# Where the plain chunks stand between the products of a Strassen-like block, norm weights stored on 128 partitions, and a load queue changed

## The chip, the cores and the metric

The kernel runs on one NeuronCore of a Trainium2 chip. The metric is the device time of one execution in microseconds (us), from the first instruction to the last with what the program needs around them. The input arrays lie in HBM in the layout that the host code prepares, and that preparation is not timed.

## The reference, cut to what matters

The reference is two transformer blocks on one sequence of 256 tokens and width 1024, in float32:

```python
x = x + 0.5 * swiglu(rms_norm(x, g), w_gate, w_up, w_down)    # width 2816, first of four such layers
...
x = x + first_mixer(rms_norm(x, g))       # sparse attention and pooling; q and k: rms_norm per head, with q_norm, k_norm
x = x + 0.5 * swiglu(...)                 # second
x = x + 0.5 * swiglu_2(...)               # third
x = x + hybrid_mixer(rmsnorm(x, g), ...)  # with a norm of its own, sgu_norm
x = x + 0.5 * swiglu_2(...)               # fourth
return rmsnorm(x, final_norm)
```

where `swiglu(h) = (silu(h @ w_gate) * (h @ w_up)) @ w_down`. The four feed-forward layers (called FFN 1 to 4 here) are most of the time.

## The kernel before, in words

**Precision.** A float32 matrix is used as two parts of a faster matmul type: `split` makes the high part by a copy on ScalarE (line 82, ACT) and the low part by a subtraction on VectorE (line 83, DVE). `mm3` (lines 88 to 90) multiplies them as hi·hi, hi·lo and lo·hi. Every weight chunk of 128x2048 values is loaded, split into tiles `whi` and `wlo` (three buffers of each, in the pool `wsp`) and used by TensorE (PE). So the split of a chunk can start only when the third chunk before it has been used.

**Plain chunks.** `weights` loads a chunk into `raw` (two buffers, SP queue), splits it, and `rows` multiplies it for both halves of the tokens: 24 matmuls of 512 columns. These results go to PSUM banks with the tag `acc` (five).

**7-product blocks.** `quad` computes a 2x2 block product (two token halves, gate and up columns, two halves of the inner dimension) with seven products in place of eight. A product is 12 matmuls of 512 columns into a PSUM bank with the tag `tmp` (three banks, which the transposes in `turned` use too). The seven are, in order of `yield`: p1 of quarter w11; p2 of w12, which holds the sum of two quarters; p3 of w22; p4 of w21; p5 of w11 with another quarter added to it; p6 after `w11 += w22` on DVE (line 198); p7 after `w11 += w21` on DVE (line 201). The sums for p2 and p5 are made by adding DMAs (`more`, line 180, POOL queue). The quarters lie in tiles `block` (four buffers) and were loaded by the POOL queue (line 156). Results of p1, p2, p3 and p5 leave PSUM by an ACT copy (line 177), the others by a DVE operation (lines 193, 199, 207). When p7 is done, a few DVE sums (204 to 207, 393), `silu` and `gated` make the layer's hidden values, which `turned` transposes on PE and splits.

**Order.** The string `ORDER` names the steps of one FFN after its first group of columns: `e` (2 plain chunks) and `4` (4 plain chunks) are groups of columns computed plainly, `a`, `b` and `c` are three 7-product blocks, 7 steps each, and `d` is the down product (13 steps: 12 chunks, the last in two). After each step, work put off by `later` may be issued. The tile framework takes the program in this order, and sets each engine's own order of instructions and the buffers when the kernel is built; engines then run their queues in order.

**The mixers.** In the first, lines 456 to 479 load tables and form `C` and `S` from `cosq`, `sinq` and the head norm `g`, which was read from a [1, 64] array and broadcast to 128 partitions by the DMA (line 467, SP queue). `sgu_norm` (line 733, POOL queue) and `final` (line 287, SP queue) were broadcast in the same way from [1, 1024].

Of the kernel before, what the change touches and what calls it, by code (L numbers as in the profile page):

```python
# [17 lines left out]
P = 128  # L18
T = 256
D = 1024  # L20
# [3 lines left out]
HD = 64  # L24
# [9 lines left out]
WARM = 14  # L34


ORDER = "eeaa4aa4a4aa4bbdbbdbbdbccdccdcdcdcdddddd"
DOWN = ((0, 0), (0, 5), (0, 4), (1, 0), (1, 5), (1, 4), (0, 1), (1, 1), (0, 2), (1, 2), (0, 3), (1, 3))


class Block:
# [108 lines left out]
        yield  # L150
        self.split(dst[:, :, 0, :], dst[:, :, 1, :], s)

    def block(self, src=None):
        b = self.blocks.tile([P, 2048], F32, tag="block", name="block")
        if src is not None:
            self.nc.gpsimd.dma_start(b, src)
        return b

    def quad(self, pool, b, x, xc):


        nc, tt = self.nc, self.nc.vector.tensor_tensor
        of_x = lambda c, t: lambda k: self.both(x[:, 4 * c + k, :, t * P : t * P + P])
        of_xc = lambda i: lambda k: self.both(xc[:, 4 * i + k, :, :])

        def product(left, w):
            ps = self.bank("tmp")
            for k in range(4):
                c = slice(k * 512, k * 512 + 512)
                self.mm3(ps, left(k), (w[0][:, c], w[1][:, c]), k == 0, k == 3)  # L170
            return ps

        p = lambda tag: pool.tile([P, 512], F32, tag=tag, name=tag)

        def copy(ps, tag):
            y = p(tag)
            nc.scalar.activation(y, ps, AF.Copy)
            return y

        more = lambda w, src: nc.gpsimd.dma_start(w, src, accum_op=ALU.add)  # L180
        (b11, b12), (b21, b22) = b
        w12 = self.block(b12)
        more(w12, b22)
        w11, w22, w21 = self.block(b11), self.block(b22), self.block(b21)
        y11 = copy(product(of_x(0, 0), self.parts(w11)), "p1")
        more(w11, b12)
        yield
        p7 = copy(product(of_xc(2), self.parts(w12)), "p7")
        yield
        y12 = copy(product(of_xc(3), self.parts(w22)), "p3")  # L190
        yield
        y21 = p("p2")
        tt(y21, product(of_x(1, 0), self.parts(w21)), y11, op=ALU.add)
        y11, v = y21, y11
        yield
        p5 = copy(product(of_xc(0), self.parts(w11)), "p5")
        yield
        tt(w11, w11, w22, op=ALU.add)  # L198
        tt(v, product(of_xc(1), self.parts(w11)), v, op=ALU.subtract)
        yield  # L200
        tt(w11, w11, w21, op=ALU.add)  # L201
        w = self.parts(w11)
        ps = product(of_x(1, 1), w)
        tt(p7, p7, v, op=ALU.add)
        tt(v, v, p5, op=ALU.add)
        tt(p5, p7, p5, op=ALU.add)
        tt(p7, ps, p7, op=ALU.subtract)
        return y11, p7, y12, v, p5
# [74 lines left out]
    def ending(self):  # L283

        nc = self.nc
        self.fg = self.block()[:, :D]
        nc.sync.dma_start(self.fg, self.a["final"].to_broadcast([P, D]))
        self.half = self.small.tile([P, 2], F32, tag="tot", name="half")
        nc.vector.tensor_scalar(self.half, self.sq[:, 0, :], 1.0 / D, EPS, op0=ALU.mult, op1=ALU.add)
        self.y = [self.block()[:, :D] for _ in range(2)]  # L290
        for t in range(2):
            nc.vector.tensor_tensor(self.y[t][:, :512], self.X[t][:, :512], self.fg[:, :512], op=ALU.mult)
# [55 lines left out]
    def ffn(self, n, following, first=False):  # L348
        nc, a = self.nc, self.a
        gu, d, d_end = a[f"gu{n}"], a[f"d{n}"], a[f"de{n}"]  # L350
        with self.stage(4), self.tc.tile_pool(name="act", bufs=1) as pool:
            act = pool.tile([P, KF, 2, T], F32R, tag="act", name="act")
            xc = pool.tile([P, 16, 2, P], F32R, tag="xc", name="xc")
# [32 lines left out]
                gated(j, sgs, [x[:, T:] for x in G] if j == 5 else U)  # L386

            def seven(j):
                y11, y21, y12, x, y22 = yield from self.quad(pool, [[gu[2 * j + i, c] for i in range(2)] for c in range(2)], self.hT, xc)

                def rest():
                    tt = nc.vector.tensor_tensor
                    tt(y12, y12, x, op=ALU.add)
                    gated(j, silu([y11, y21]), [y12, y22])

                self.later(rest, 3)
# [40 lines left out]
            next(combined)  # L437

            steps = {"a": seven(1), "b": seven(2), "c": seven(3), "4": eight(4), "e": eight(5), "d": down()}
            for step in ORDER:  # L440
                next(steps[step], None)
# [14 lines left out]
    def mixer1_tables(self):  # L456
        nc, a, c1 = self.nc, self.a, self.c1
        load = lambda name, shape, engine=None: self.load(c1, name, shape, engine)
        self.cosi, self.sini = load("cosi", [P, 2, 32]), load("sini", [P, 2, 32])
        cosq, sinq = load("cosq", [P, 2, 64]), load("sinq", [P, 2, 64])  # L460
        self.causal, self.ncausal = load("causal", [P, 2, T], nc.gpsimd), load("ncausal", [P, 2, T], nc.gpsimd)
        self.band, self.pw = load("band", [P, 4, 384], nc.gpsimd), load("pool_w", [P, 4, P], nc.gpsimd)
        self.pscale = load("pool_scale", [P, 4], nc.gpsimd)
        self.heads_of = {}
        for n in ("q", "k"):
            g = c1.tile([P, HD], F32, tag=f"{n}g", name=f"{n}g")
            nc.sync.dma_start(g, a[f"{n}_norm"].to_broadcast([P, HD]))
            self.heads_of[n] = (cosq, sinq, g)

    def tables_of(self, n):  # L470
# [258 lines left out]
    def mixer2_tables(self):  # L729
        load = lambda name, shape: self.load(self.c2, name, shape, self.nc.gpsimd)  # L730
        self.sw, self.sb, self.cw = load("sgu_w", [P, 8, P]), load("sgu_b", [P, 8]), load("conv_w", [P, 8, 3])
        self.sn = self.c2.tile([P, D], F32, tag="sn", name="sn")
        self.nc.gpsimd.dma_start(self.sn, self.a["sgu_norm"].to_broadcast([P, D]))

    def mixer2(self, following):
        nc, a, m2 = self.nc, self.a, self.m2
# [127 lines left out]
    def load(self, pool, name, shape, engine=None):  # L864
        t = pool.tile(shape, F32, tag=name, name=name)
        (engine or self.nc.sync).dma_start(t, self.a[name])
        return t
# [70 lines left out]
def _layout(i):  # L938
    i = {k: np.asarray(v) for k, v in i.items()}
    one = {k: (v[0] if k not in ("x", "final_norm_2") else v) for k, v in i.items()}  # L940
    out = {"x": i["x"][0].reshape(2, P, D), "xT": i["x"][0].T.reshape(KD, P, T).transpose(1, 0, 2)}
    downs = [one["ffn1_w_down"], one["ffn2_w_down"], one["ffn1_w_out_2"], one["ffn2_w_out_2"]]
    gates = [(one[f"ffn{s}_w_gate"], one[f"ffn{s}_w_up"]) for s in "12"]
    gates += [(w[:, :FF], w[:, FF:]) for w in (one["ffn1_w_in_2"], one["ffn2_w_in_2"])]
    for n, (gu, w) in enumerate(zip(gates, downs), 1):
        out[f"gu{n}"] = _gate_up(*gu)
        out[f"d{n}"] = _chunks(w[: 20 * P])
        out[f"de{n}"] = np.stack([_by_rows(w[20 * P :, f * 512 : f * 512 + 512], 2)[0] for f in range(2)])
    w = one["w_in"]
    q, k, v, qi, ki, wi, u = np.split(w, np.cumsum([512, 512, 512, 256, 64, 4]), axis=1)  # L950
    out["w_idx"] = _by_rows(np.concatenate([qi, ki, wi], 1), 4)
    for n, m in (("q", q), ("k", k), ("v", v), ("u", u)):
        out[f"w_{n}"] = _by_rows(m, 4)
    out["w_out"] = np.concatenate([_chunks(one["w_out"][:512])[:, 0], _chunks(one["w_out"][512:])[:, 0]])
    out["pool_w"] = one["pool_w"].transpose(1, 0, 2)
    out["pool_scale"] = one["pool_scale"].reshape(4, P).T
    w = one["w_in_2"]
    u, v, gb, gc, xb, ga, gbb = np.split(w, 7, axis=1)
    for n, m in (("w_v2", v), ("w_u2", u), ("w_ga2", ga), ("w_gb2", gbb), ("w_pa2", one["w_proj_a_2"]),
                 ("w_pb2", one["w_proj_b_2"]), ("w_out_2", one["w_out_2"])):  # L960
        out[n] = _chunks(m)
    out["w_b2"] = _by_tile(gb).reshape(4, 2, P, D).transpose(0, 2, 1, 3).reshape(4, P, 2 * D)
    out["w_cx"] = _by_tile(gc, xb)
    out["sgu_w"] = one["sgu_w_2"].transpose(2, 0, 1)
    out["sgu_norm"] = one["sgu_norm_2"].reshape(1, D)
    out["sgu_b"] = one["sgu_b_2"].T
    out["conv_w"] = one["conv_w_2"].reshape(3, 8, P).transpose(2, 1, 0)
    out["final"] = one["final_norm_2"].reshape(1, D)
    out["gains"] = np.concatenate([one[n].reshape(KD, P).T for n in NORMS], 1)
    for n in ("q_norm", "k_norm"):  # L970
        out[n] = one[n].reshape(1, HD)
    return {k: np.ascontiguousarray(v) for k, v in out.items()}


# [9 lines left out]
```

## Time and profile before

| | us |
|---|---|
| median of 3 runs (lowest, highest) | 1111.79 (1111.42, 1115.6) |
| the profiled execution | 1109.44 |
| its span, first to last instruction | 1107.7 |
| PE busy in the span | 1067.8 (96%) |
| DVE busy | 818.4 (74%) |
| ACT busy | 605.3 (55%) |
| mean granted TensorE clock | 0.989 |

The profiled execution lies 2.35 us below the median, and its span 1.74 us below its own time. "Busy" of PE counts matmuls whose ends are modelled and which overlap, so what PE loses is read from the distance of matmul starts and from the idle times that the rows name.

### The profile page before, as it was taken

The numbers are of one execution on the slowest core, as the hardware profiler recorded it, in microseconds if no ns is written. First come the engines' busy times: TensorE is split into PE (matmuls) and PEld (weight loads), VectorE is DVE, ScalarE is ACT, GpSimd is POOL, SyncE is SP. The second block draws the span as 40 slices with busy tenths as digits, with TensorE's granted clock in tenths as the row PEclk, the third lists the DMA queues.
The fourth block names the chain that finished last, engine by engine and source line by source line (L and its number), as shares of the span: only waits on it lengthen the run. The fifth ranks groups of instructions, "written<-read, shape, count | busy, mean of one in ns | idle before, by whom it ended". The sixth has DMA issues, their size and how long they took to land.

```text
span 1107.7 us, 12935 instructions
## 1 busy us (share of the span) xinstructions
PE 1067.8 (96%) x5134; PEld 882.3 (80%) x5134; DVE 818.4 (74%) x827; ACT 605.3 (55%) x685; POOL 66.3 (6%) x109
## 2 busy tenths in 40 slices
PE   9999899999999989999998999999999999998996
PEld 7778678778888768788876878999888888877875
DVE  6778986696676988867688866777555567787884
ACT  6665654576456656455565445533444455564552
POOL 0100000110010100001010000000000001010000
PEclk9999999999999999999999999999999999998998
DMA  9977636722397766469686475465445439776542
GB/s 347 329 231 216 208 123 260 250 102 104 118 351 216 226 192 188 154 251 326 186 246 195 130 290 199 153 206 178 179 168 184 155 147 326 221 232 202 178 155 73
DMA packets 36108, 226.93 MB, mean 205 GB/s; under 512 B 4736, under 2 KB 5136, under 8 KB 10448
## 3 DMA queue, kind: packets, MB, share of 16 engines
q1 hardware_dynamic: 24336, 147.16, 36.4%
q0 software_dynamic: 11136, 78.14, 24.5%
q8 instruction: 40, 0.66, 0.2%
q10 hardware_dynamic: 576, 0.82, 0.2%
q14 instruction: 20, 0.16, 0.0%
HBM read 225.05 MB, written 1.05 MB: 204 GB/s over the span
## 4 chain that ended last, share of the span: by engine, by line
PE 67%; DVE 17%; ACT 7%; issue 6%; DMA 3%; SPq 0%; ACTq 0%; POOLq 0%; POOL 0%; DVEq 0%
PE acc L89 14%; PE acc L90 14%; PE acc L88 14%; DVE wlo L83 9%; PE tmp L89 7%; PE tmp L90 7%; PE tmp L88 7%; ACT whi L82 6%; DVE block L198 2%; DVE block L201 2%; PE acc L96 1%; PE tmp L216 1%; DMA xT<-in_xT 1%; DVE pr L368 1%; DMA raw<-in_d 1%
## 5 line engine op out<-in xcount | busy, mean ns | idle before, releaser
L83 DVE TENSOR_TENSOR wlo<-block,whi 128x2048 fp32r<-128x2048 f32 (+2 forms) x127 | 262.0, 2074 | 93.7 <-ACT whi L82 93.5
L83 DVE TENSOR_TENSOR wlo<-raw,whi 128x2048 fp32r<-128x2048 f32 (+1 forms) x111 | 245.5, 2212 | 110.7 <-ACT whi L82 110.5
L82 ACT ACTIVATE whi<-raw 128x2048 fp32r<-128x2048 f32 (+1 forms) x111 | 205.0, 1851 | 172.2 <-PE acc L90 78.6
L82 ACT ACTIVATE whi<-block 128x2048 fp32r<-128x2048 f32 (+2 forms) x127 | 219.9, 1741 | 126.6 <-DVE block L201 55.7
L88 PE MATMUL acc<-whi,hT 128*128 128x512 f32 (+1 forms) x432 | 168.0, 392 | 5.0 <-ACT whi L82 4.9
L89 PE MATMUL acc<-wlo,hT 128*128 128x512 f32 (+1 forms) x432 | 168.6, 390 | 2.5 <-DVE wlo L83 2.5
L90 PE MATMUL acc<-whi,hT 128*128 128x512 f32 (+1 forms) x432 | 167.3, 388 | 2.6 <-DVE hT L229 2.6
L88 PE MATMUL acc<-whi,act 128*128 128x512 f32 x352 | 137.8, 401 | 8.8 <-ACT whi L82 8.5
L89 PE MATMUL acc<-wlo,act 128*128 128x512 f32 x352 | 138.6, 394 | 2.1 <-DVE wlo L83 1.8
L90 PE MATMUL acc<-whi,act 128*128 128x512 f32 x352 | 137.7, 391 | 0.0
L88 PEld LDWEIGHTS acc<-whi,hT 128*128 128x128 f32 x432 | 81.4, 189 | 24.2 <-ACT whi L82 7.0
L89 PEld LDWEIGHTS acc<-wlo,hT 128*128 128x128 f32 x432 | 81.7, 189 | 20.1 <-DVE wlo L83 4.1
L90 PEld LDWEIGHTS acc<-whi,hT 128*128 128x128 f32 x432 | 81.6, 189 | 19.2 <-DVE hT L229 3.1
L89 PE MATMUL tmp<-wlo,hT 128*128 128x512 f32 x240 | 94.4, 393 | 0.0
L88 PE MATMUL tmp<-whi,hT 128*128 128x512 f32 x240 | 94.3, 395 | 0.0
L90 PE MATMUL tmp<-whi,hT 128*128 128x512 f32 x240 | 93.6, 390 | 0.0
L88 PEld LDWEIGHTS acc<-whi,act 128*128 128x128 f32 x352 | 65.8, 190 | 26.3 <-ACT whi L82 13.7
L88 PE MATMUL tmp<-whi,xc 128*128 128x512 f32 x192 | 77.1, 402 | 7.0 <-ACT whi L82 5.9
L89 PEld LDWEIGHTS acc<-wlo,act 128*128 128x128 f32 x352 | 66.6, 189 | 18.3 <-DVE wlo L83 4.9
L90 PEld LDWEIGHTS acc<-whi,act 128*128 128x128 f32 x352 | 66.6, 189 | 13.8
L89 PE MATMUL tmp<-wlo,xc 128*128 128x512 f32 x192 | 77.1, 401 | 0.0
L90 PE MATMUL tmp<-whi,xc 128*128 128x512 f32 x192 | 76.2, 397 | 0.0
(267 smaller groups left out, 1506.1 us busy)
## 6 DMA issues: line engine op xcount, KB each, us to landing
block<-in_gu POOLq DMA_DIRECT2D x72, 1024.0 KB, 7.7
raw<-in_d SPq DMA_DIRECT2D x40, 1024.0 KB, 4.8
raw<-in_gu SPq DMA_DIRECT2D x36, 1024.0 KB, 5.6
raw<-in_de SPq DMA_DIRECT2D x8, 512.0 KB, 3.8
block<-in_w_out SPq DMA_DIRECT2D x4, 1024.0 KB, 4.9
raw<-in_w_out SPq DMA_DIRECT2D x4, 1024.0 KB, 5.4
block<-in_w_cx SPq DMA_DIRECT2D x4, 1024.0 KB, 5.0
raw<-in_w_cx SPq DMA_DIRECT2D x4, 1024.0 KB, 4.9
```

The lines of the kernel that those rows point to most:

```text
L82: self.nc.scalar.activation(hi, x, AF.Copy)
L83: self.nc.vector.tensor_tensor(lo, x, hi.bitcast(F32), op=ALU.subtract)
L88: mm(ps, lhsT=a[0], rhs=b[0], start=start, stop=False)
L89: mm(ps, lhsT=a[0], rhs=b[1], start=False, stop=False)
L90: mm(ps, lhsT=a[1], rhs=b[0], start=False, stop=stop)
L96: self.nc.tensor.matmul(ps, lhsT=a, rhs=b, start=start, stop=stop)
L198: tt(w11, w11, w22, op=ALU.add)
L201: tt(w11, w11, w21, op=ALU.add)
L216: self.nc.tensor.transpose(pt[:, i, :], x[t][:, i * P : i * P + P], self.ident)
L368: nc.vector.scalar_tensor_tensor(pr, us[t], r[:, t : t + 1], sgs[t], op0=ALU.mult, op1=ALU.mult)
```

## The change

Three edits. `ORDER` is another string: in each 7-product block the first four products now follow each other, and plain chunks stand between p4, p5, p6, p7 and after p7. The numbers of steps are the same. One chunk of the down product moves from block c to block b. In FFN 1 alone, the four first quarters of block a (`j == 1`) are loaded by the SP queue in place of the POOL queue; the adding DMAs stay on POOL. The four norm vectors are stored on 128 rows, and their DMAs read [128, n] arrays without a broadcast.

```diff
-ORDER = "eeaa4aa4a4aa4bbdbbdbbdbccdccdcdcdcdddddd"
+ORDER = "eeaaaa4a4a4a4bbbbdbdbdbdccccdcdcdcdddddd"
...
-    def block(self, src=None):
+    def block(self, src=None, queue=None):
         b = self.blocks.tile([P, 2048], F32, tag="block", name="block")
         if src is not None:
-            self.nc.gpsimd.dma_start(b, src)
+            (queue or self.nc.gpsimd).dma_start(b, src)
         return b
...
-        w12 = self.block(b12)
+        w12 = self.block(b12, queue)
         more(w12, b22)
-        w11, w22, w21 = self.block(b11), self.block(b22), self.block(b21)
+        w11, w22, w21 = self.block(b11, queue), self.block(b22, queue), self.block(b21, queue)
...
-        nc.sync.dma_start(self.fg, self.a["final"].to_broadcast([P, D]))
+        nc.sync.dma_start(self.fg, self.a["final"])
...
-                y11, y21, y12, x, y22 = yield from self.quad(pool, [[...]], self.hT, xc)
+                y11, y21, y12, x, y22 = yield from self.quad(pool, [[...]], self.hT, xc, nc.sync if first and j == 1 else None)
...
-            nc.sync.dma_start(g, a[f"{n}_norm"].to_broadcast([P, HD]))
+            nc.sync.dma_start(g, a[f"{n}_norm"])
...
-        self.nc.gpsimd.dma_start(self.sn, self.a["sgu_norm"].to_broadcast([P, D]))
+        self.nc.gpsimd.dma_start(self.sn, self.a["sgu_norm"])
...
-    out["sgu_norm"] = one["sgu_norm_2"].reshape(1, D)
+    out["sgu_norm"] = np.tile(one["sgu_norm_2"].reshape(1, D), (P, 1))
...
-    out["final"] = one["final_norm_2"].reshape(1, D)
+    out["final"] = np.tile(one["final_norm_2"].reshape(1, D), (P, 1))
...
-        out[n] = one[n].reshape(1, HD)
+        out[n] = np.tile(one[n].reshape(1, HD), (P, 1))
```

## Rows read from the trace of the kernel before

**Rows 1.** The page's busy times: us, share of the span, instructions.

```profile
PE 1067.8 (96%) x5134; PEld 882.3 (80%) x5134; DVE 818.4 (74%) x827; ACT 605.3 (55%) x685; POOL 66.3 (6%) x109
```

**Rows 2.** PE's groups by line and shape: busy us, mean ns, idle before, releasers.

```profile
L88 PE MATMUL acc<-whi,act 128*128 128x512 f32 x352 | 137.8, 401 | 8.8 <-ACT whi L82 8.5
...
L88 PE MATMUL tmp<-whi,xc 128*128 128x512 f32 x192 | 77.1, 402 | 7.0 <-ACT whi L82 5.9 <-ACT p L177 1.0
```

**Rows 3.** PE's timeline in FFN 2: start, duration, and idle time before in brackets.

```profile
309.20 0.39 PE L90 MATMUL acc<-whi,hT 128*128 128x512 f32 x1
309.43 0.39 PE L88 MATMUL acc<-whi,hT 128*128 128x512 f32 x1
```

**Rows 4.** PE's timeline in FFN 2, end of block a, and p6 of block b.

```profile
367.09 0.39 PE L88 MATMUL tmp<-whi,hT 128*128 128x512 f32 x1
368.50 0.73 PE L88 MATMUL acc<-whi,hT 128*128 128x512 f32 x2 [1.03 <-ACT whi L82]
...
400.75 0.39 PE L90 MATMUL tmp<-whi,xc 128*128 128x512 f32 x1
402.62 0.50 PE L88 MATMUL tmp<-whi,xc 128*128 128x512 f32 x1 [1.48 <-ACT whi L82]
404.90 0.50 PE L88 MATMUL acc<-whi,act 128*128 128x512 f32 x1 [1.78 <-ACT whi L82]
```

**Rows 5.** PE's timeline in FFN 2, p6 and p7 of block c.

```profile
444.50 0.39 PE L88 MATMUL tmp<-whi,xc 128*128 128x512 f32 x1
444.96 0.73 PE L88 MATMUL acc<-whi,act 128*128 128x512 f32 x2
...
453.12 0.39 PE L88 MATMUL tmp<-whi,hT 128*128 128x512 f32 x1
453.73 0.73 PE L88 MATMUL acc<-whi,act 128*128 128x512 f32 x2 [0.22 <-ACT whi L82]
```

**Rows 6.** DVE's timeline in FFN 2, block b: sum and split of p6, sum of p7.

```profile
398.26 2.28 DVE L198 TENSOR_TENSOR block<-block 128x2048 f32<-128x2048 f32 x1
402.60 2.29 DVE L83 TENSOR_TENSOR wlo<-block,whi 128x2048 fp32r<-128x2048 f32 x1 [2.06 <-ACT whi L82]
...
407.09 2.28 DVE L201 TENSOR_TENSOR block<-block 128x2048 f32<-128x2048 f32 x1
```

**Rows 7.** Stretches after block b's stall, FFN 3 and 4: busy by engine, clock, DMA.

```profile
590.50:594.50 4.00, 2.98 (x7) 2.40 (x8) 4.00 (x3) 0.96 (x1) 0.00 (x0) 0.57 0.40 170
...
1015.50:1021.00 5.50, 5.33 (x13) 4.17 (x14) 4.65 (x3) 0.88 (x2) 0.31 (x1) 0.50 0.41 143
```

**Rows 8.** The stretch from block a's p7 into block b, FFN 2 (columns: PE, PEld, DVE, ACT, POOL).

```profile
366.70:389.60 22.90, 21.79 (x99) 16.84 (x98) 22.90 (x19) 14.63 (x13) 2.81 (x4) 1.00 0.82 255
```

**Rows 9.** Timelines in FFN 2: p2 of block a on PE, and ACT and DVE there.

```profile
337.01 0.50 PE L88 MATMUL tmp<-whi,xc 128*128 128x512 f32 x1 [0.23 <-ACT p L177]
...
336.36 0.60 ACT L177 ACTIVATE p<-tmp 128x512 f32<-128x512 f32 x1 [0.31 <-PE tmp L90]
...
337.32 1.28 DVE L83 TENSOR_TENSOR act<-tmp,act 128x512 fp32r<-128x512 f32 x2
```

**Rows 10.** DMA issues in the first mixer: KB, us to landing; then DVE's and PE's timeline there.

```profile
sinq<-in_sinq SPq DMA_DIRECT2D x1, 64.0 KB, 5.6
qg<-in_q_norm SPq DMA_DIRECT2D x1, 32.0 KB, 7.8
...
205.22 0.29 DVE L475 TENSOR_TENSOR qC<-cosq,qg 128x128 f32<-128x128 f32 x1 [5.19 <-DMA qg<-in_q_norm]
...
208.30 0.41 PE L90 MATMUL acc<-whi,hT 128*128 128x324 f32 x1 [2.57 <-DVE hT L229]
```

**Rows 11.** DMA landing: FFN 1's second adding DMA; down chunks, median; FFN 3's slowest.

```profile
block<-in_gu POOLq DMA_DIRECT2D x1, 1024.0 KB, 17.2
...
raw<-in_d SPq DMA_DIRECT2D x40, 1024.0 KB, 4.8
...
raw<-in_d SPq DMA_DIRECT2D x1, 1024.0 KB, 9.7
```

More of the change, by code (lines that the diff above doesn't have):

```diff
@@ L151, in combined, with quad @@
         self.split(dst[:, :, 0, :], dst[:, :, 1, :], s)
-    def block(self, src=None):
+    def block(self, src=None, queue=None):
         b = self.blocks.tile([P, 2048], F32, tag="block", name="block")
         if src is not None:
-            self.nc.gpsimd.dma_start(b, src)
+            (queue or self.nc.gpsimd).dma_start(b, src)
         return b
-    def quad(self, pool, b, x, xc):
+    def quad(self, pool, b, x, xc, queue):
         nc, tt = self.nc, self.nc.vector.tensor_tensor
@@ L388, in seven @@
             def seven(j):
-                y11, y21, y12, x, y22 = yield from self.quad(pool, [[gu[2 * j + i, c] for i in range(2)] for c in range(2)], self.hT, xc)
+                y11, y21, y12, x, y22 = yield from self.quad(pool, [[gu[2 * j + i, c] for i in range(2)] for c in range(2)], self.hT, xc, nc.sync if first and j == 1 else None)
                 def rest():
```

## Prediction

> **What bounds the kernel now.** I read the page first: PE is busy 96% of the span, DVE 74%, ACT 55% [rows 1]. So PE's own work is the floor, and a change of order can give back only what PE waits for. I then asked for PE's groups with the idle time before them: the first matmul of an `mm3` waits for `whi` from ACT, 8.5 us in all ahead of chunks with `act`, 5.9 us ahead of products with `xc` [rows 2]. These idle times count from modelled ends, so I took starts from the timeline: full speed is one matmul of 512 columns per 0.23 us [rows 3]. A product (12 matmuls) is then 2.7 us of PE, a plain chunk (24) 5.4 us. Any longer distance is lost.
>
> In FFN 2 the losses stand at three places. Block a: p7's first matmul starts at 367.09, the next matmul at 368.50; 1.41 less the 0.23 is 1.18 us. Block b: 400.75, 402.62 and 404.90, so 1.64 + 2.05 = 3.69 us around p6 [rows 4]. Block c: 0.46 - 0.23 and 0.61 - 0.23, together 0.61 us [rows 5]. The same waits recur in all four FFNs: four times 1.48 us is the 5.9 us of rows 2, and four times 1.78 is 7.1 of the 8.5 there.
>
> Why block b is worst is seen on DVE. p6 needs, one after another, the sum of line 198 (2.28 us), the ACT copy (DVE idles 2.06 us for it), and the low part (2.29 us): 398.26 to 404.89, 6.6 us. p7 needs the same again from 407.09 [rows 6]. PE has 2.7 us of work in a product. Before, p6 stood right behind p5 in block b, and p7 right behind p6 in block a. Block c, whose order before was already p5, chunk, p6, chunk, p7, loses 0.61.
>
> After block b's stall in FFN 3 and 4 the granted clock falls to a mean of 0.57 over 4.0 us and 0.50 over 5.5 us [rows 7], the lower level of 1.2 GHz. In the second stretch PE issues 13 matmuls, 13 x 0.23 = 3.0 us at full speed, so 2.5 us are lost; in the first 7, 1.6 us, so 2.4 are lost, of which I leave half to the stall that runs into it. Together 3.7 us; I take 3.6.
>
> **The change, step by step.**
>
> *Order, blocks a and b.* The stalls go: 4 x (1.18 + 3.69) = 19.5 us, and with them the 3.6 us of clock. In their place stands block c's pattern, as both blocks now have a chunk ahead of p5, p6 and p7. From p6's start to p7's start PE has 2.7 + 5.4 = 8.1 us of work against the chain of 6.6. I charge block c's 0.61 to the two blocks in four FFNs: 8 x 0.61 = 4.9 us. The bounds are 0 and this, as in block c DVE puts two plain splits ahead of the sums and still loses no more.
>
> *Order, p1 to p4 in a row.* This is new; before, two at most stood together. Three buffers of `whi` mean that p4's split starts at p1's end and has p2 and p3 to hide in, 5.4 us. It needs an ACT copy of p1's result if that is queued ahead (0.60) [rows 9], the high part (2.06 with handing over) and the low (2.29) [rows 6]: 4.95 us, which leaves 0.45. Anything that DVE does in between (a sum, `gated`, a transposed piece) comes out of that. DVE has no idle time at the seam of a and b even now: 22.90 of 22.90 us busy from 366.7, while PE is busy for 21.79 [rows 8]. In that stretch the end of block a, C4 (its last chunk) and p1 to p4 of b will meet. It helps that p7 of a is now split earlier, as its chain starts one chunk sooner, so DVE enters the seam with a lead of a few us. The nearest row for a product behind a product is p2 of block a: PE idles 0.23 us on the ACT copy that frees its bank [rows 9]. I take 0.3 us for each of 12 blocks, 3.6 us; bounds 0 and 2.6 us a block (below).
>
> *Order, loads.* In the new order p3 and p4 come up to 5.4 us earlier after p1, and p5 one chunk earlier. In rows 2 no group of products waits for a DMA. In FFN 1, where loads are slowest, block a's second adding DMA takes 17.2 us [rows 11]. p5's split is due p2, p3, p4 and a chunk (13.5 us) after p1, plus what DVE was ahead with p1's own split (one product and one chunk at least), less its own split (4.35, as above): 17.2 us. It just fits, with nothing to spare; I price it 0, bounds 0 and 5.4 once. For the blocks b and c the sums that free the tiles come earlier, so their loads do too. The one chunk of the down product that moves from c to b needs only hidden values that are ready after blocks e and 4, so 0.
>
> *First quarters on SP.* Four issues of one FFN move from POOL to SP. They are of plain data and on PE's path only if late; on SP they stand between the plain chunks' loads, and a quarter that waits for its tile then holds the next `raw` load behind it. No wait for either is among PE's in rows 2: 0, with the 5.4 above as the bound for this edit too.
>
> *Norm weights.* `qg` was issued 0.48 us behind `sinq` and landed 7.8 us after its issue, against 5.6 for `sinq` with twice the bytes. DVE stood 5.19 us for it with a split and the parts of `hT` behind, and PE then waited 2.57 us for `hT` [rows 10]. Without the broadcast I take `sinq`'s 5.6: 2.2 us sooner, nearly all of PE's wait, so 2.1 us gained; bounds 0 (the queue was full and bytes are the same) and 2.6. `sgu_norm` and `final` gate no wait that I found: 0.
>
> Sum: -19.5 - 3.6 + 4.9 + 3.6 - 2.1 = -16.7 us. The profiled execution would go from 1109.4 to 1092.7; it lies 2.35 below the median of the runs, so the median goes from 1111.8 to **1095.1 us**, 1.5% faster. A measurement of this kernel tells about 0.5% (5.6 us) from no change.
>
> **The rivals.**
>
> *Better (0.13).* Block c's pattern loses nothing where DVE is not loaded with transposes, four in a row cost nothing, and FFN 3's down chunk is no longer late: its `raw` load took 9.7 us where a usual one takes 4.8, as the next mixer's loads ran beside it [rows 11], which I put at 4.9 us of lateness, some 4 of it on PE. 19.5 + 3.6 + 2.1 + 4 is 29 us: 1083. Against it: those loads start when block c's last tile is free, and that end of the order is the same.
>
> *The stall only moves to p3 and p4 (0.15).* At the seams DVE does one piece of leftovers, such as the low parts of a transposed pair (1.28 us) [rows 9], in front of a low part that PE needs, in every block. 12 x 1.3 = 15.6 in place of 3.6: 12 us of the gain is lost, 1107. Rows 8 speak for it, DVE's lead against it.
>
> *The order as written is not the order as run (0.10).* The framework orders each engine's queue itself; in rows 4 and 5 two matmuls of the next chunk stand inside a product. If it again lets the low part of a chunk go ahead of the sums of p6, block b stalls as before and only `qg`'s 2.1 us come: 1110, no change.
>
> *Slower (0.10): the three `tmp` banks.* With four products in a row no chunk on `acc` banks hides the emptying of a bank, and `turned` takes two of the three banks in the midst (after p2 in a and b). If the ACT copy that frees one stands behind a high part (2.06 us with handing over [rows 6]) and half of a transposed pair's low parts (0.64) [rows 9] behind that, a block loses 2.7 us less what hides, I take 2.6, in place of the stall. The gain to be eaten is 19.5 + 3.6 + 2.1 - 4.9 = 20.3 us, so from 1.7 us a block on the change loses; at 2.6 it is 31 - 20.3, or 10.9 us slower: 1123. Rows 9 show the mechanism at 0.23 us, an eighth of that.
> The Trainium skill, "Perfetto Trace Analysis", section "Optimizing Tensor Performance", has matmul groups rotate through PSUM banks so that emptying one overlaps the next group's matmuls; four short groups on three shared banks are what it warns of. By that rule alone this case would be the likelier; rows 9 agree that the bank is waited for, but put it at 0.23 us, and I follow the row.
>
> **How the numbers follow.** Forecast 0.52, better 0.13, moved stall 0.15, order not run 0.10, banks 0.10. Faster by over 0.5%, below 1106.2: the forecast, the better case, and near half of the moved stall, 0.72 in all. Within 0.5%: the rest of the moved stall and the order case, 0.19. Slower: 0.09. The range reaches from the better case, 1083, to the moved stall, 1108, and leaves out the order and the bank cases; the forecast's own range, with four in a row at 0 to 0.9 us a block and block c's pattern at 0 to 0.61, is 1086 to 1103.
>
> **What would show it.** Right: in blocks a and b no idle of over 0.5 us at p6 and p7; the idle for `whi` in rows 2 falls from 14.4 to some 3 us; no stretch at clock 0.50 in FFN 3 and 4 apart from the late chunk; `qg` lands in under 6 us. Wrong: new idle times at p3 or p4 on the ACT copy (banks) or on `wlo` (DVE), once per block; in FFN 1, PE idle on a `block` that a DMA fills; p6's sum on DVE behind a plain chunk's low part with PE waiting.

## The result, and the profile after

The changed kernel takes 1084.69 us (median of 4 runs, 1082.18 to 1087.56) against 1112.2 us for the kernel before in the same comparison: a ratio of 0.9748, 95% interval 0.9715 to 0.978. It is 2.5% faster, inside the prediction's whole range (1083 to 1108), but 1.3 us below the range that it gave for its own forecast (1086 to 1103): the gain is 27 us where the forecast had 16.7. The profiled execution of the changed kernel took 1087.56 us (span 1085.3), the slowest of its four.

The page's busy times, and PE's groups with the idle time before them, the counterparts of [rows 1, 2]:

```profile
PE 1061.3 (98%) x5134; PEld 884.0 (81%) x5134; DVE 819.7 (76%) x827; ACT 603.9 (56%) x685; POOL 64.5 (6%) x105
```

```profile
L88 PE MATMUL acc<-whi,act 128*128 128x512 f32 x352 | 137.4, 396 | 1.4 <-ACT whi L82 1.0
...
L88 PE MATMUL tmp<-whi,xc 128*128 128x512 f32 x192 | 76.1, 396 | 3.3 <-ACT p L177 3.3
```

The idle for `whi`, 14.4 us in [rows 2], is 1.0. In its place products wait 3.3 us for the ACT copy that empties a `tmp` bank; that was 1.0. PE's busy time is 6.5 us less with the same 5134 matmuls.

The view of all of PE's waits begins with what is left (total, times, longest):

```profile
PE acc L89 <- DVE wlo L83: 3.6, 3, 1.8
PE acc L90 <- DVE hT L229: 3.3, 1, 3.3
PE tmp L88 <- ACT p L177: 3.3, 8, 0.8
```

PE's timeline at p6 and p7 of block b in FFN 2, where [rows 4] had gaps of 1.64 and 2.05 us, with DVE's timeline of the sum and split of p6 behind it:

```profile
398.21 0.39 PE L88 MATMUL tmp<-whi,xc 128*128 128x512 f32 x1
...
406.37 0.39 PE L88 MATMUL tmp<-whi,hT 128*128 128x512 f32 x1
406.60 0.41 PE L88 MATMUL acc<-whi,act 128*128 128x512 f32 x1
407.03 0.50 PE L89 MATMUL tmp<-wlo,hT 128*128 128x512 f32 x1
```

```profile
391.46 2.28 DVE L198 TENSOR_TENSOR block<-block 128x2048 f32<-128x2048 f32 x1
395.80 2.29 DVE L83 TENSOR_TENSOR wlo<-block,whi 128x2048 fp32r<-128x2048 f32 x1 [2.06 <-ACT whi L82]
```

The chain of p6 still takes 6.6 us (391.46 to 398.09), as in [rows 6]. But its sum now begins 1.3 us before PE's p5 (392.77), while PE is still in the chunk ahead of p5, and PE comes to p6 at 398.21, just as the chain ends: p6 starts at full pace, 0.22 us behind the matmul before it. At p7 one start is 0.43 us from the next in place of 0.23: 0.20 us is lost. In block a nothing is lost at either product. In block c the distances are 0.50 and 0.64 us, 0.27 and 0.41 lost, much as in [rows 5].

What is lost follows the lead, the time from the start of the sum on DVE to the time at which PE comes to the product. The chain needs 6.6 us; the table has FFN 2 of both profiles, read from the starts in the timelines:

| product | sum starts | PE is there | lead | lost |
|---|---|---|---|---|
| before: b's p6 | 398.26 | 400.98 | 2.7 | 3.69 |
| before: a's p7 | 362.35 | 367.09 | 4.7 | 1.18 |
| changed: c's p7 | 440.61 | 446.14 | 5.5 | 0.41 |
| changed: c's p6 | 431.87 | 437.52 | 5.7 | 0.27 |
| changed: b's p7 | 400.33 | 406.37 | 6.0 | 0.20 |
| changed: b's p6 | 391.46 | 398.21 | 6.8 | 0 |
| changed: a's p7 | 358.01 | 366.00 | 8.0 | 0 |
| changed: a's p6 | 349.16 | 357.84 | 8.7 | 0 |

The new waits stand in block a of FFN 2, at p2 and p3 (one wait of 0.23 in [rows 9]):

```profile
334.94 0.50 PE L88 MATMUL tmp<-whi,xc 128*128 128x512 f32 x1 [0.69 <-ACT p L177]
...
338.65 0.50 PE L88 MATMUL tmp<-whi,xc 128*128 128x512 f32 x1 [0.25 <-ACT p L177]
```

Four stretches of 6 us behind block b's p6 or p7, one in each FFN, run at full clock (stretch, its length, PE's busy time and matmuls, granted clock, DMA share, GB/s):

```profile
118.00:124.00 6.00, 5.98 (x26) 1.00 0.76 280
400.00:406.00 6.00, 6.00 (x28) 1.00 0.47 157
582.00:588.00 6.00, 6.00 (x28) 1.00 0.55 180
998.50:1004.50 6.00, 6.00 (x28) 1.00 0.61 201
```

In this execution the head norm got worse. The DMA issue of `qg` in mixer 1, then PE's timeline there, the counterparts of [rows 10]:

```profile
qg<-in_q_norm SPq DMA_DIRECT2D x1, 32.0 KB, 8.4
```

```profile
205.40 0.64 PE L90 MATMUL acc<-whi,hT 128*128 128x324 f32 x1 [3.32 <-DVE hT L229]
```

Without the broadcast `qg` lands in 8.4 us, not in 7.8, and PE waits 3.32 us, not 2.57. That is one execution: in the five other kernels below that have the vectors on 128 rows and the tables where they were, `qg` lands in 7.0 to 7.8 us and PE waits 1.8 to 2.6; in the five with the broadcast it is 7.6 to 8.0 and 2.4 to 2.8. Behind the wait the clock is low, and so it is in FFN 1, where SP's queue carries the first quarters (windows, PE alone):

```profile
33.00:37.00 4.00, 3.02 (x7) 0.57 1.03 279
204.00:208.00 4.00, 2.60 (x9) 0.53 0.48 147
208.00:212.00 4.00, 4.00 (x18) 0.62 0.42 141
```

For the comparisons below the span is cut into six stages at the starts of `rstd` (line 103), so that a loss can be put to a stage; us, one profiled execution each. FFN 1 includes the start, FFN 4 the end. One stage can differ by up to 3 us between kernels that are the same there: mixer 1, the same in the changed kernel, `e2_norms`, `e7_sgu`, `e8_nosp` and `e9_sums`, takes 103.7 to 106.8.

| kernel | FFN 1 | mixer 1 | FFN 2 | FFN 3 | mixer 2 | FFN 4 |
|---|---|---|---|---|---|---|
| before | 198.8 | 105.2 | 186.8 | 191.4 | 232.8 | 192.7 |
| changed | 195.1 | 106.8 | 182.2 | 184.5 | 231.7 | 184.9 |
| order alone | 192.3 | 105.4 | 182.0 | 185.6 | 232.8 | 185.5 |
| changed, less SP edit | 193.2 | 103.7 | 182.0 | 183.5 | 231.7 | 185.5 |

### The profile page after: what moved, and what is told of

Same layout as the page of the kernel before. It is cut to its first block, busy times and chain, and to the rows that moved or that the text cites. A ratio compares the mean times of both kernels' runs of the same rounds, so it can differ in the third digit from the quotient of the medians.

```text
span 1085.3 us, 12947 instructions
## 1 busy us (share of the span) xinstructions
PE 1061.3 (98%) x5134; PEld 884.0 (81%) x5134; DVE 819.7 (76%) x827; ACT 603.9 (56%) x685; POOL 64.5 (6%) x105
## 4 chain that ended last, share of the span: by engine, by line
PE 82%; DVE 7%; ACT 4%; DMA 3%; issue 3%; SPq 0%; POOL 0%; POOLq 0%; ACTq 0%; DVEq 0%
PE acc L88 16%; PE acc L90 16%; PE acc L89 16%; PE tmp L88 10%; PE tmp L89 10%; PE tmp L90 10%; DVE wlo L83 4%; ACT whi L82 3%; DMA raw<-in_d 1%; PE acc L96 1%; PE tmp L216 1%; DMA xT<-in_xT 1%; DVE block L198 1%; DVE block L201 1%; DMA qg<-in_q_norm 1%
## 5 line engine op out<-in xcount | busy, mean ns | idle before, releaser
L88 PE MATMUL tmp<-whi,xc 128*128 128x512 f32 x192 | 76.1, 396 | 3.3 <-ACT p L177 3.3
L90 PE MATMUL tmp<-whi,xc 128*128 128x512 f32 x192 | 74.9, 390 | 0.0
```

Source lines behind the costliest of these rows:

```text
L88: mm(ps, lhsT=a[0], rhs=b[0], start=start, stop=False)
L90: mm(ps, lhsT=a[1], rhs=b[0], start=False, stop=stop)
```

## The experiments

**Order alone** (`e1_order`): the kernel before with the new `ORDER`.

```diff
-ORDER = "eeaa4aa4a4aa4bbdbbdbbdbccdccdcdcdcdddddd"
+ORDER = "eeaaaa4a4a4a4bbbbdbdbdbdccccdcdcdcdddddd"
```

> The new ORDER alone; norms and queue as before. Theory (the order is the whole gain): FFN 2, from rstd to rstd, goes from 186.8 to about 182.2 us as in the changed kernel; no wait of over 0.5 us at p6 and p7 of blocks a and b; FFN 1 up to the first mixer's rstd is shorter than the changed kernel's 195.1 by about 2 us, as the quarters stay on POOL; the median is 24 to 30 us below the kernel before. Rival (the other two edits carry part of it): the median is less than 22 us below.

Measured: 1086.42 us, ratio 0.9773 (0.9757 to 0.979), 25 us faster. The order is nearly the whole gain. FFN 2's stage and the waits at p6 and p7 are those of the changed kernel.

**Norm weights alone** (`e2_norms`): the kernel before with the vectors stored on 128 rows.

```diff
-            nc.sync.dma_start(g, a[f"{n}_norm"].to_broadcast([P, HD]))
+            nc.sync.dma_start(g, a[f"{n}_norm"])
...
-        out[n] = one[n].reshape(1, HD)
+        out[n] = np.tile(one[n].reshape(1, HD), (P, 1))
```

> The norm vectors on 128 rows alone. Theory (the DMA queues are full when q_norm is asked for, so the broadcast never was the cause): q_norm lands 7.5 to 8.5 us after its issue as before, PE waits 2.5 to 3.5 us for hT there, time within 2 us of before. Rival (the prediction's term): it lands in under 6 us, PE's wait falls to about 0.5 us, 2 us faster.

Measured: ratio 1.0002 (0.9984 to 1.002). `qg` lands in 7.0 us and PE's wait is 1.79 us, not 2.57, which no time shows. So the broadcast was at most a small part of what made `qg` late.

**SP's quarters alone** (`e3_sp`): the kernel before with block a's first quarters in FFN 1 on SP's queue.

```diff
-        w12 = self.block(b12)
+        w12 = self.block(b12, queue)
...
-        w11, w22, w21 = self.block(b11), self.block(b22), self.block(b21)
+        w11, w22, w21 = self.block(b11, queue), self.block(b22, queue), self.block(b21, queue)
...
```

> The first quarters of FFN 1's block a on the SP queue alone, old ORDER and broadcast norms. Theory (SP's place costs at FFN 1's start, as in the changed kernel): PE loses 4 to 5 us between 28 and 40 us, against 2.5 before; the time to the first mixer's rstd grows from 198.8 by 1 to 2.5 us. Rival (the quarters were late on POOL): it falls.

Measured: ratio 1.0028 (1.0012 to 1.0043), 1 to 5 us slower. Its first stage is 204.6 us against 198.8, more than the 1 to 2.5 expected; part of that is a granted clock of 0.51 from 32 to 39 us, which the profile before doesn't have there. This edit costs.

**The change without it** (`e8_nosp`).

```diff
-... self.hT, xc, nc.sync if first and j == 1 else None)
+... self.hT, xc, None)
```

> The changed kernel with all first quarters on POOL again. Theory (the SP edit costs): the time to the first mixer's rstd falls from 195.1 to 193 or 194 us, no other stage moves. Rival (the new order needs the SP queue in FFN 1, as p3 and p4 come earlier): PE waits for a block filled by a DMA in FFN 1's block a, and that time grows.

Measured: 1082.74 us, ratio 0.9747 (0.9732 to 0.9761), 2.0 us below the changed kernel, with runs that overlap (1081.62 to 1084.78 against 1082.18 to 1087.56). FFN 1 takes 193.2 us, 1.9 less than in the changed kernel. The issues on SP are the likely reason: in the changed kernel the four quarters stand on the queue from 17.20 to 30.76 us between two pairs of `raw` loads, and the second pair goes out at 33.95 and 36.16; before, it went out at 31.60 and 33.86, here at 30.82 and 34.92. But PE's waits there are no longer for it: between 29 and 35 us PE idles 2.4 us in the changed kernel (for `whi`, for a transposed piece and for `wlo`) and 2.7 us here. What differs is the clock behind them, 0.57 from 33 to 37 us in the changed kernel and 1.00 here, and `e7_sgu`, without the edit, has low clock there too. So that the edit costs is shown by `e3_sp`; how much of the 1.9 us is its own is not.

Two stages that this edit doesn't touch are shorter as well, mixer 1 by 3.1 us and FFN 3 by 1: PE waits 2.0 us for `hT` in place of 3.3, with the clock at 1.00 behind it, and 0.8 us for a late chunk of the down product in place of 1.8. From the order alone to this kernel the time falls by 3.7 us, and between the two kernels stand only the norm vectors, whose edit was worth nothing in the old order; whether it is worth something in the new one no run settles. The four that follow start from this kernel.

**Four `tmp` banks** (`e5_banks`): four banks of each tag in place of three `tmp` and five `acc`.

```diff
-... bufs={"acc": 5, "tmp": 3}[tag])
+... bufs={"acc": 4, "tmp": 4}[tag])
...
-        return self.bank("acc" if self.banks % 8 < 5 else "tmp", shape)
+        return self.bank("acc" if self.banks % 8 < 4 else "tmp", shape)
```

> The changed kernel without its SP edit, and with four tmp banks and four acc banks in place of three and five. Theory (p2 and p3 wait for a tmp bank that the ACT copy must empty): PE's idle on the copy, 3.3 us over 8 waits, falls to 1 or less, 2 to 4 us faster than the same kernel with three banks. Rival (the copy is late in ACT's own queue whatever the banks, or the acc banks get short): the waits stay or move to acc, no gain or slower.

Measured: 1081.4 us (1080.85 to 1081.72), ratio 0.9713 (0.9686 to 0.9741). No wait for the copy of line 177 is left, and FFN 2, 3 and 4 are 2.0, 1.4 and 1.65 us shorter. FFN 1 is 4.0 longer: PE stands there once, for 5.4 us, until ACT's `sg` (line 360) frees an `acc` bank.

So the waits at p2 and p3 are waits for a bank. The Trainium skill, "Perfetto Trace Analysis", section "Optimizing Tensor Performance", asks for groups that rotate through different banks, so that emptying one overlaps the next group's matmuls; that section names no number of banks, and that four groups on three banks are too few was the prediction's reading of it. The trace agrees, for both tags: a fourth `tmp` bank takes 3.3 us of waits away, and the `acc` bank given for it costs one of 5.4.

**Mixer 1's tables behind `qg`** (`e6_tables`): `causal`, `ncausal`, `band` and `pool_w` (1.5 MB) and the small `pool_scale` by SP's queue behind the head norms, not by POOL's beside them.

```diff
-        self.causal, self.ncausal = load("causal", [P, 2, T], nc.gpsimd), load("ncausal", [P, 2, T], nc.gpsimd)
-        self.band, self.pw = load("band", [P, 4, 384], nc.gpsimd), load("pool_w", [P, 4, P], nc.gpsimd)
-        self.pscale = load("pool_scale", [P, 4], nc.gpsimd)
...
             nc.sync.dma_start(g, a[f"{n}_norm"])
             self.heads_of[n] = (cosq, sinq, g)
+        self.causal, self.ncausal = load("causal", [P, 2, T]), load("ncausal", [P, 2, T])
+        self.band, self.pw = load("band", [P, 4, 384]), load("pool_w", [P, 4, P])
+        self.pscale = load("pool_scale", [P, 4])
```

> The changed kernel without its SP edit, and with the five big tables of the first mixer asked for on the SP queue behind q_norm and k_norm, in place of the POOL queue beside them. Theory (q_norm lands late because the DMA engines are full with those 1.5 MB): it lands in under 5 us, PE's wait for hT falls from 2 to under 0.5 us, the stage from the mixer's rstd to the next one shrinks by 1.5 to 4 us. Rival (the small rows themselves are slow): it lands in about 7 us as before, no gain.

Measured: 1078.27 us, ratio 0.9686 (0.9659 to 0.9713). `qg` lands in 3.7 us, DVE waits 1.21 us for it, PE for nothing, and mixer 1's stage falls from 103.7 to 100.7 us:

```profile
qg<-in_q_norm SPq DMA_DIRECT2D x1, 32.0 KB, 3.7
```

So `qg` was late because 1.5 MB of tables moved beside it; `e11_combo` and `e12_banks`, with the same edit, have it in 3.5 and 4.0 us.

**Mixer 2's tables on SP** (`e7_sgu`): the same for `sgu_w`, `sgu_b`, `conv_w` and `sgu_norm`, which POOL issues in the midst of FFN 3's last down chunks.

```diff
-        load = lambda name, shape: self.load(self.c2, name, shape, self.nc.gpsimd)
+        load = lambda name, shape: self.load(self.c2, name, shape, self.nc.sync)
...
-        self.nc.gpsimd.dma_start(self.sn, self.a["sgu_norm"])
+        self.nc.sync.dma_start(self.sn, self.a["sgu_norm"])
```

> The changed kernel without its SP edit, and with the second mixer's tables (sgu_w, sgu_b, conv_w, sgu_norm) on the SP queue. Theory (FFN 3's last down chunks come late because these 1 MB from the POOL queue take the DMA engines from them): the chunk lands in 5 to 7 us, the 2.0 us gap of PE near the end of FFN 3 goes. Rival (the next weights on SP do it): the chunk still takes over 8 us.

Measured: 1081.62 us, ratio 0.9715 (0.9683 to 0.9748). FFN 3's stage goes from 183.5 to 181.2 us and its wait for the late chunk, 1.79 us of idle in the changed kernel and 0.81 in the one without the SP edit, is gone; mixer 2 gives 0.8 back. Against the 1082.74 that is 1.1 us, with runs that overlap; `e11_combo` below shows the gain clear of them.

**Sums ahead of the chunk** (`e9_sums`): the sums of lines 198 and 201 written right behind the product that frees their tile, to remove block c's 0.27 and 0.41.

```diff
         p5 = copy(product(of_xc(0), self.parts(w11)), "p5")
-        yield
         tt(w11, w11, w22, op=ALU.add)
-        tt(v, product(of_xc(1), self.parts(w11)), v, op=ALU.subtract)
         yield
+        tt(v, product(of_xc(1), self.parts(w11)), v, op=ALU.subtract)
         tt(w11, w11, w21, op=ALU.add)
+        yield
         w = self.parts(w11)
```

> The changed kernel without its SP edit, and with the two sums of a block written right behind the product that frees w11, ahead of the plain chunk's split. Theory (block c still loses 0.6 us as DVE puts the chunk's low part ahead of the sum): block c's gaps at p6 and p7 go, 4 x 0.6 = 2.4 us, and no other gap grows by more. Rival (what binds there is DVE's total work, not its order): the gaps stay or move to the chunk behind.

Measured: 1083.6 us, ratio 0.9733 (0.9705 to 0.976): no gain on the 1082.74. p7's gap in c goes, and a new one opens at c's p6 in all four FFNs, 1.34 us of idle for `whi` in FFN 2.

**Block a's order alone** (`e4_a_only`).

```diff
-ORDER = "eeaa4aa4a4aa4bbdbbdbbdbccdccdcdcdcdddddd"
+ORDER = "eeaaaa4a4a4a4bbdbbdbbdbccdccdcdcdcdddddd"
```

> The kernel before with only block a's part of the order new (eeaaaaa4a4a4a4bbdbbdbbdb...). Theory (a gap at p6 or p7 belongs to the block in which products stand side by side): in FFN 2 a's 1.18 us goes, b's 3.69 us and the low clock behind it in FFN 3 and 4 stay; four FFNs times 1.18 is 4.7 us, less 0.3 a block for four products in a row (1.2): about 3.5 us faster, ratio 0.997. Rival (the two blocks share one backlog on DVE, so a's earlier chain also eases b): b's gap shrinks below 3 us and the ratio goes to 0.990 or less.

(The expectation prints one `a` too many; the line above is what ran.) Measured: 1107.17 us against 1113.59, ratio 0.9943 (0.9922 to 0.9965), 6.4 us faster. Block a's 1.18 us is gone, and p2 and p3 of a show the waits of 0.69 and 0.25 us of the changed kernel. Block b's two gaps are 1.64 and 2.05 us in FFN 2, as before, so a's earlier chain did not ease b and the rival falls. The gain is larger than a's own gaps give; the span, 1104.3, is 3.4 us shorter, as expected, and the rest lies between executions: the clock is low behind b's gaps in all four FFNs here.

**The old order with early sums** (`e10_oldsums`): the edit of `e9_sums`, the two sums one `yield` earlier, in the kernel before.

```diff
         p5 = copy(product(of_xc(0), self.parts(w11)), "p5")
-        yield
         tt(w11, w11, w22, op=ALU.add)
-        tt(v, product(of_xc(1), self.parts(w11)), v, op=ALU.subtract)
         yield
+        tt(v, product(of_xc(1), self.parts(w11)), v, op=ALU.subtract)
         tt(w11, w11, w21, op=ALU.add)
+        yield
         w = self.parts(w11)
```

> The kernel before, old order, with the two DVE sums of p6 and p7 written right behind the product that frees their tile, ahead of the chunk between. Theory (p6 and p7 are late as the sum, the copy and the low part take 6.6 us against 2.7 us of PE's work between products that stand side by side): b's gap at p6 stays, as its sum stood right behind p5 already; a's 1.18 at p7 may shrink: ratio 0.995 to 1.002. Rival (the sums were late only because chunks' low parts were ahead of them on DVE): b's 3.69 us and a's 1.18 us both go, 19.5 us, ratio 0.982.

Measured: 1108.1 us, ratio 0.9955 (0.9932 to 0.9977). Block a's gap is gone: the sum for p6 now runs ahead of a chunk's low part, and the lead at p7 grows from 4.7 to 5.8 us. b's p6 in FFN 2 has the idle times of [rows 4] to the hundredth, 1.48 and 1.78, and c's p6 gains a wait:

```profile
444.64 0.50 PE L88 MATMUL tmp<-whi,xc 128*128 128x512 f32 x1 [1.30 <-ACT whi L82]
```

That b's gaps stay is no test of the rival for block b, because the edit moves nothing ahead of p6 there: its sum stood right behind p5 already. DVE's timeline of the kernel before settles it. Ahead of the sum at 398.26 it has p5's own low part and the short operation of line 193, and no chunk's:

```profile
395.45 2.29 DVE L83 TENSOR_TENSOR wlo<-block,whi 128x2048 fp32r<-128x2048 f32 x1 [2.53 <-ACT whi L82]
```

So in block b, with products side by side, a chain of 6.6 us has 2.7 us of PE's work to hide behind, and only work between them helps. In block a the place in DVE's queue counted as well.

**Both table edits** (`e11_combo`): `e6_tables` and `e7_sgu` together.

> The changed kernel with first quarters on their old queue, and the tables of both mixers loaded by the SP queue (both single edits together). If the two gains are separate they add: 3.0 us in mixer 1's stage and 2.3 us in FFN 3's, against 1082.7: about 1077.4, ratio 0.968. Rival (one of them was the granted clock's scatter): FFN 3's stage stays at 183.5 us or mixer 1's at 103.7, and the time at 1079 to 1081.

Measured: 1076.55 us, ratio 0.967 (0.964 to 0.97); mixer 1 100.7, FFN 3 181.2. The gains add, and with `e6_tables`' 1078.27 (1077.92 to 1078.78) as its base the second one is clear of the runs' spread (1075.57 to 1077.17).

**And four banks** (`e12_banks`): `e11_combo` with four banks of each tag, FFN 1's first plain group on `tmp` banks.

```diff
-... bufs={"acc": 5, "tmp": 3}[tag])
+... bufs={"acc": 4, "tmp": 4}[tag])
...
-        return self.bank("acc" if self.banks % 8 < 5 else "tmp", shape)
+        return self.bank("acc" if self.banks % 8 < 4 else "tmp", shape)
...
-            two = lambda: [self.bank("acc") for _ in range(2)]
+            two = lambda tag="acc": [self.bank(tag) for _ in range(2)]
...
-                G = two()
+                G = two("tmp" if first and j == 5 else "acc")
```

> The same with four tmp and four acc banks, and in FFN 1 the first group of plain chunks on tmp banks. Theory: the waits of products for the copy that frees a bank (3.3 us over 8) go, FFN 2 to 4 are each 1.4 to 2 us shorter as with four and four alone, and the one 5.4 us wait of FFN 1 does not come: about 1072, ratio 0.963. Rival: with one acc bank fewer, FFN 1 or a mixer waits for a bank elsewhere; then its stage is 2 to 4 us longer and the time 1075 to 1078.

Measured: 1070.73 us (1069.29 to 1071.37), ratio 0.9614 (0.9588 to 0.964), the fastest here. FFN 1 keeps its 193.2, mixer 1 its 100.7; against `e11_combo` FFN 2, 3 and 4 are 1.3, 0.4 and 1.7 us shorter and mixer 2 is 1.0. PE is busy 99% of the span, and its longest wait is one of 1.6 us for `wlo`.

## Why the prediction was right, and where its sizes were off

The mechanism was right and was the likeliest case of the text: the stalls at p6 and p7 go because PE has other work while the chain runs. The order alone gives 25 us; with a's order alone a's gap goes and b's stays; and what is lost follows the lead. The time, though, lies beside the better rival's 1083, and that nearness is luck: of what that rival changed in the sum (block c's pattern at nothing, four in a row at nothing, the late chunk gone) only the first came near. The terms, from the two profiled executions, each rounded from starts in the timelines:

| step of the prediction | forecast | measured |
|---|---|---|
| stalls of a and b at p6 and p7 | -19.5 | -19.5 |
| low clock behind b | -3.6 | -3.9 in this execution; 7 to 9 in others |
| block c's pattern in a and b | +4.9 | +0.8 (0.20 in b alone, four times) |
| four products in a row | +3.6 | +2.9 (0.85 to 1.2 in FFN 2 to 4, 0 in FFN 1) |
| `qg` | -2.1 | +1.6 (mixer 1's stage): 0.75 of PE's wait, the rest low clock behind it |
| loads and SP's quarters | 0 | +1.9 (FFN 1, against the kernel without them, low clock included) |
| FFN 3's late chunk | a rival, not in the sum | -2.0 |
| small gaps of 0.22 to 0.35 in block b | not seen | -1.6 |

They add up to -19.8; the span fell by 22.4. Of the 2.6 left over mixer 2 has 1.1, and no run settles where these come from.

**A half chunk that the text did not see.** It gave PE 5.4 us in the chunk between two products. In block b the chunk between p5 and p6 is the half one of the down product, 12 matmuls from 395.49 to 397.99. With p5 that is 5.4 us of work against the chain of 6.6; p6 held because DVE was 1.3 us ahead, and with 0.1 us to spare. Between p6 and p7 the 8.1 us are there, but the sum begins 2.1 us into them, behind two low parts on DVE, and 0.20 us is lost.

**Low clock, the largest miss.** The prediction read the clock from one execution, in which it fell behind b's stall in FFN 3 and 4 only. Four other kernels here keep that stall. The same windows of 6 us behind it, of the kernel with the norm weights alone:

```profile
114.29:120.29 6.00, 6.00 (x20) 0.72 0.37 120
405.01:411.01 6.00, 6.00 (x21) 0.76 0.33 123
592.93:598.93 6.00, 6.00 (x14) 0.50 0.32 111
1016.55:1022.55 6.00, 6.00 (x15) 0.52 0.36 125
```

A window at full clock has 27 matmuls behind this stall. Here 7, 6, 13 and 12 are missing: 38 x 0.23 is 8.7 us. In the three others it is 7.1, 7.8 and 8.0 us, in the profiled execution of before (27, 27, 21 and 16) 3.9. So the profiled execution of before lost little here, and its time, 2.35 us below the median, fits that. The kernel before's 39 later executions agree: the four with a mean granted clock of 0.983 took 1116.3 to 1116.9 us, the seven with 0.990 or more 1107.6 to 1111.6. With the stall gone none of this is left. From one profiled execution to the other the time fell by 21.9 us; with the 2.35 on this side and 2.87 on the other, where the changed kernel's profiled execution lies above its median, this makes the 27.1 from 1111.79 to 1084.69. The prediction knew of the 2.35 and added it to the changed kernel too, but what made it, as far as these runs show, goes with the stall.

**Block c's pattern.** The charge of 0.61 for a and b was a guess from the nearest row, and its lower bound, 0, was nearer. Block b loses 0.20 and a nothing, where the lead is longer: between p5's low part and p6's sum DVE has in block a one plain split, in b a transposed piece and the half chunk's split, in c a transposed piece and a whole split.

**Four products in a row.** Near the sum forecast, and at the place the text named, the ACT copy that frees a `tmp` bank. That the sum came out is partly luck: it had 0.3 us in each of 12 blocks, and three of them, block a in FFN 2 to 4, carry nearly all. That this is a bank and no late split is shown by `e5_banks`. The bank rival (1123 us) had the mechanism, but at 0.85 to 1.2 us an FFN, nearly all in block a, not at 2.6 in each block.

**`qg`: the step that failed.** "Without the broadcast I take `sinq`'s 5.6" laid the delay to the broadcast. Without it `qg` took 7.0 to 8.4 us in six kernels, and 3.7 in `e6_tables`: it was the tables on POOL's queue. The lower bound of the text said so ("the queue was full and bytes are the same") and should have been the value.

**SP's quarters.** Priced 0, with the very mechanism named, "holds the next `raw` load behind it". The edit alone cost 3 us (`e3_sp`, ratio 1.0028), in the changed kernel some 2; the bound of 5.4 held for the time.

**The late chunk.** The better rival had it, as going entirely. In the changed kernel's profile it went by half: the low clock behind it is gone and 2.03 us stay. But in `e1_order`, with the same order, it stands whole (idle of 0.56 and 1.82 us, then a clock of 0.50 to 646), as in the kernel before (0.43 and 1.83), so the order did not take it away. Over the kernels that load the tables by POOL the longest of these waits goes from none to 1.83 us. It goes with mixer 2's tables on SP's queue.

## What to carry to other kernels

Where a product needs a chain of sum, high part and low part, write the chain's length beside PE's work ahead of it, and put independent work between until the second is longer. Moving the sum earlier in its queue works only where something stands ahead of it, and can cost the next block: here it freed block a of its 1.18 us (`e10_oldsums`), and block c got a wait of 1.3 for it in both kernels that had it. Look at every small load that an engine waits for together with all that moves beside it on other queues, and count the banks whenever short groups are put side by side. A stall that is followed by low clock can cost more in the median than in the one profile at hand, as it did here: look at it in several executions.

## What the runs showed of the hardware

Behind two waits of 1.64 and 2.05 us, with one matmul between them, the mean granted clock of the next 6 us was 0.50 to 0.77 at 17 of the 20 places at which five kernels with the old block b were looked at, so for some 3 to 6 of the 6 us TensorE ran at its lower level, 1.2 GHz; at the other three it was 1.00. The same kernel shows it in one FFN and not in the next. A wait of 3.3 us for `hT` in mixer 1 had low clock behind it (0.53 and 0.62 over 8 us); one of 2.0 us there had a clock of 1.00 behind it in `e8_nosp` (204 to 212 us) and of 0.50 in `e5_banks` (207 to 210 us).

`qg`, a load of 32 KB, landed in 7.0 to 8.4 us in the 11 kernels in which 1.5 MB on another queue went beside it, and in 3.5 to 4.0 us in the three in which that came behind it on its own queue. Whether one row was broadcast to 128 partitions or 128 rows were read made little of that: 7.6 to 8.0 us in five kernels, 7.0 to 8.4 in six.
